# More of the first expert product ahead of the second, and one index lookup per route

## The chip, the cores and the metric

One program runs on one core of a Trainium2 chip. Times are device microseconds (us). TensorE (PE in the profile) multiplies matrices, VectorE (DVE) and ScalarE (ACT) work elementwise, GpSimd (POOL) issues gathers, and SyncE (SP) issues most transfers. Each engine works through its own list of instructions in order. A "tile" below is one weight block of 128 x 1024 float32, 512 KB.

## The reference

256 tokens of width 1024 pass two blocks of two layers each. The second block ends each layer with a layer of 16384 experts of which each token takes 8 x 16:

```python
q = (h @ w_pq).reshape(B, L, 8, 2, 128)
s = einsum("blhpd,hpkd->blhpk", q, peer_keys)       # 8 heads, 2 halves, 128 keys
sv, si = lax.top_k(s, 16)
cand = sv[..., 0, :, None] + sv[..., 1, None, :]     # 16 x 16 sums of a head
top_s, pos = lax.top_k(cand, 16)
eidx = take_along_axis(si0 * 128 + si1, pos)         # expert numbers
gate = softmax(top_s)
a = peer_down[eidx] @ h                              # first product, per expert
act = gate * gelu(a)
out = act @ peer_up[eidx]                            # second product
```

All else (retention, state-space scan, attention, pooling, Fourier mixing, feed-forward) is left alone by the change.

## The kernel before, in words

For the x tokens the expert layer is computed densely: all 128 tiles of `peer_down` (a *down* tile is 128 experts times 256 tokens, 24 matmuls), then gelu, then times a gate matrix that is zero for experts not chosen, then all 128 tiles of `peer_up` (an *up* tile, 24 matmuls that add to eight accumulators). This is `peer_dense(l)` from line 1549, once in each layer. For the context tokens of layer 0 the chosen rows are gathered instead (`peer_jobs`).

Every weight tile passes `Stream.run`: SP loads it into one of 4 stage buffers (line 338), ACT rounds it to a high half (line 314), DVE subtracts to get the low half (line 315, the *split*), and three matmuls per 128-row block multiply (lines 471 to 473). Splits are emitted up to three tiles ahead of the step that uses them. Beside the tiles run *background jobs* in lanes: each job carries a cost in steps, each step earns its lane a credit of 1, and jobs are emitted while the credit pays. When a lane is ended (`bg_end`), what is left is emitted at once. This gives the order in which instructions are emitted. From it and the dependencies the framework's scheduler fixes, at compile time, the order of each engine's list; it may move an instruction forward when it is ready and those emitted earlier are not.

In `peer_dense` the order of steps is: 16 tiles of `w_pq` (`dense_front`, line 1347), with the scores of a head after each pair; then AHEAD = 56 down tiles (line 1642 is their gelu); then pairs of one up and one down tile until all down tiles are done; then up tiles alone. In layer 0 the tiles of the next modulation are mixed into the up phase (`st.fill`).

The background jobs in lane 1 make the gate matrix. They are, in this order of emission: 8 *routes* of the first 128 tokens (one per head, `route`, line 1432, five jobs each at a cost of 0.4: two top-16 searches, the 16 x 16 sums with their own top 16, two lookups); a softmax and a transpose (lines 1575 and 1584); 32 *fours* (line 1587, cost 0.35: four one-hot matrices and one comparison on DVE at lines 1596 and 1598, then a product on PE at line 1604, copied by ACT at line 1605) mixed with the 8 routes of the other 128 tokens; then softmax, transpose and 32 fours for those. After each fourth four ACT sends 1 MB of gates to DRAM (line 1607). All have to be there before up tile 0: SP reads the gates back for eight tiles at a time (line 1647), `prep` multiplies them into a down result (line 1653) and makes its halves (lines 478 and 479).

The lookup in a route finds, for each of 16 chosen places, the key number in a list of 16: compare with 0..15 (line 1469), multiply by the numbers (line 1470), sum (lines 1473 and 1477), once for each half, after two conversions from integer (lines 1456 and 1465).

A down result needs a *slot* of 128 x 256 until its up tile; there are 56 in parts of other buffers. The halves of `prep` go into the first blocks of `y2`, the second operand of other stages, idle here.

Of the kernel before, what the change touches and what calls it, by code (L numbers as in the profile page):

```python
# [10 lines left out]
F32 = mybir.dt.float32  # L11
# [118 lines left out]
def dense_units(down, up):  # L130

    d = down.reshape(128, 128, 8, 128).transpose(0, 3, 2, 1).reshape(128, 128, 1024)
    u = up.reshape(128, 128, 1024)
    order = [d[i] for i in range(AHEAD)]
    for i in range(128):
        order += [u[i]] + ([d[i + AHEAD]] if i + AHEAD < 128 else [])
    return units(order)

# [29 lines left out]
N_ARENA = 14336  # L168
AHEAD = 56

# [193 lines left out]
def tile_model(ctx: ExitStack, tc: tile.TileContext, a: dict, out: bass.AP):  # L364
# [32 lines left out]
    def take(side, dtype=F32R):  # L397
        if dtype is F32R:
            place[side] = operands.tile([128, 2, NB, T], F32R, name=side, tag=side)
        else:  # L400
            place[side] = operands.tile([128, NB, T], F32, name=side + "f", tag=side)
    take("x2")
# [11 lines left out]
    gsm = keep.tile([128, DEPTH, 2, 2, NB], F32, name="gsm")  # L414
    ckv2 = keep.tile([128, 2, 2, T], F32R, name="ckv2")
    ckvh, ckvl = ckv2[:, 0], ckv2[:, 1]
# [8 lines left out]
    gates = keep.tile([128, 2, SLOTS], F32, name="gates")  # L425
    scratch = keep.tile([128, 512], F32, name="scratch")
    fgain = keep.tile([128, NB], F32, name="fgain")
# [603 lines left out]
    def modulation(l, c0, c1):  # L1031

        held = {}
        for i in range(4 * c0, 4 * c1):
            def go(w, oc=i // 4, kq=i % 4):
                if kq == 0:
                    held[0] = md_pool.tile([128, 512], F32, name="md")
                o = held[0][:4, :]
                for kk in range(2):
                    s, c = slice(kk * 512, (kk + 1) * 512), sc_s[:, 2 * kq + kk]  # L1040
                    PE.matmul(o, c, w[:, 0, s], start=kq == 0 and kk == 0, stop=False)
                    PE.matmul(o, c, w[:, 1, s], start=False, stop=kq == 3 and kk == 1)
                if kq == 3:
                    row = scratch[:4]
                    S.activation(row, o, AF.Copy)

                    def turn():
                        p = stat(8).rearrange("p (a b) -> p a b", b=2)
                        for j in range(4):
                            PE.matmul(p[:, j], row[:, j * 128:(j + 1) * 128], sel, start=True, stop=True)  # L1050
                        V.tensor_add(mods[:, l, oc * 4:oc * 4 + 4], p,
                                     bc(P("b_mod", l * 48 + oc * 4, 4)[:, :, None], [128, 4, 2]))
                    st.later(2, turn)
            st.w(go, (a[f"mod{l}"], i))
# [378 lines left out]
    def route(tt, hd, last=None, xi=None):  # L1433
# [3 lines left out]
        def part(o, *shape):  # L1437
            return shaped(scratch[:, o:], shape)
        sv, sif, siu = part(0, 2, 16), part(32, 2, 16), part(64, 2, 16).bitcast(U32)
        hs = slice(16 * hd, 16 * hd + 16)  # L1440
        e = part(112, 16)
        ts = part(96, 16) if xi is None else xi[:, 2, tt, hs]
        pu, au = part(128, 16).bitcast(U32), part(144, 2, 16).bitcast(U32)
        af, i12, zs = part(176, 2, 16), part(208, 2, 16), part(240, 1)
        cand, cf = part(256, 16, 16), part(256, 256)
        sq = [128, 16, 16]

# [7 lines left out]
        def pairs16():  # L1455
            put(V.tensor_copy(sif, siu))
            V.tensor_tensor(cand, bc(sv[:, 0][:, :, None], sq), bc(sv[:, 1][:, None, :], sq), op=OP.add)
            best16(ts, pu, cf)

            if xi is None:  # L1460
                V.tensor_scalar(e, ts, ts[:, 0:1], None, op0=OP.subtract)
                S.activation(e, e, AF.Exp, accum_out=zs)
            V.tensor_scalar(au[:, 0], pu, 4, None, op0=OP.logical_shift_right)
            V.tensor_scalar(au[:, 1], pu, 15, None, op0=OP.bitwise_and)
            V.tensor_copy(af, au)
            lookup(0)

        def lookup(half):
            V.tensor_tensor(cand, bc(af[:, half][:, :, None], sq), bc(iota16[:, None, :], sq), op=OP.is_equal)
            V.tensor_tensor(cand, cand, bc(sif[:, half][:, None, :], sq), op=OP.mult)  # L1470

        def chosen():
            put(V.tensor_reduce(i12[:, 0] if xi is None else xi[:, 0, tt, hs], cand, AX.X, OP.add))
            lookup(1)

        def gate():
            put(V.tensor_reduce(i12[:, 1] if xi is None else xi[:, 1, tt, hs], cand, AX.X, OP.add))
            if xi is None:
                V.scalar_tensor_tensor(idx[:, tt, hs], i12[:, 0], 128.0, i12[:, 1], op0=OP.mult, op1=OP.add)
                V.reciprocal(zs, zs)  # L1480
                V.tensor_scalar(gates[:, tt, hs], e, zs, None, op0=OP.mult)
        return [lambda: top(0), lambda: top(1), pairs16, chosen, gate]

# [74 lines left out]
    def peer_dense(l, filler=None, rate=0.0, between=None, middle=None):  # L1558
# [6 lines left out]
        hot = [shaped(w[:, 1024 * i:], (2, 4, 128)) for w in (AR, AR[:, 10240:]) for i in range(2)]  # L1565
        slots = [w[:, o:o + 256] for w in (AR[:, 2048:8192], flat(h2), flat(acc), rowbuf[3], AR[:, 12288:])
                 for o in range(0, w.shape[1], 256)]
        gd = nc.dram_tensor(f"gates{l}", (16, 128, 128, 16), F32, kind="Internal").ap()
# [47 lines left out]
        def routes(hd, tt):  # L1616
            return [(0.4, f, "") for f in route(tt, hd, None, xi)]

        def blocks(tt):
            return [(0.25, lambda: softmax(tt), ""), (1.0, lambda: turn(tt), "")] + [  # L1620
                (0.35, lambda b=b, g=g: four(b, g), "") for b in range(8 * tt, 8 * tt + 8) for g in range(4)]
        late = []
# [12 lines left out]
        def act(i):  # L1635
            return shaped(slots[i % AHEAD], (16, 16))

        def down(i):
            def go(w):
                p = mm(T)  # L1640
                proj(p, w)
                S.activation(slots[i % AHEAD], p, AF.Gelu_apprx_tanh)
            return go
# [5 lines left out]
        def prep(i):  # L1649
            if i % 8 == 0 and i < 120:  # L1650
                load(i // 8 + 1)
            w, f = act(i), slots[i % AHEAD]
            V.tensor_mul(w, w, held[i // 8][:, :, i % 8, :])
            halves(yh[:, i % 3], yl[:, i % 3], f)

        def up(i):
# [6 lines left out]
            def block(i, d, w):  # L1663
                s = slice(d * 128, d * 128 + 128)
                mm3(held["acc"][d // 2][:, d % 2], w[:, 0, s], w[:, 1, s], y2[:, :, i % 3],
                    i == 0 and d % 2 == 0, i == 127)
# [19 lines left out]
            return go if i < 126 else end  # L1686
        for i in range(AHEAD):
            if i == 24 and middle:
                middle()
            st.w(down(i), (W, i))  # L1690
        st.bg_end(1)
        k = AHEAD
        if filler:
            st.fill(filler, rate)
        for i in range(128):
# [3 lines left out]
            if i == 126:  # L1699
                st.w(up(i), (W, k), (W, k + 1))  # L1700
                break
            st.w(up(i), (W, k))
            k += 1
            if i + AHEAD < 128:
                st.w(down(i + AHEAD), (W, k))
                k += 1

# [141 lines left out]
```

## Time and profile before

| | |
|---|---|
| median of 3 runs | 4310.1 us (4305.79 to 4321.45) |
| profiled execution, and its span | 4318.26 us, 4316.5 us |
| mean granted TensorE clock | 0.968 of full |
| busy: PE, DVE, ACT, POOL | 4028.0, 3375.7, 2107.0, 383.0 us |
| share of the chain that ended last: PE, DVE, DMA | 58%, 29%, 5% |
| HBM | 966.94 MB read, 36.70 MB written |

Busy time of PE counts overlapped matmuls by their modelled ends, so that a PE which is starved for half of a gap can still look busy; the number of matmul records in a stretch says more.

### The profile page before, as it was taken

To read this page: it belongs to the slowest core of one execution; us is meant where nothing else is said; L and a number is where in the kernel's file an instruction comes from. 1 tells how busy PE (TensorE), PEld (TensorE's weight loads), DVE (VectorE), ACT (ScalarE), POOL (GpSimd) and SP (SyncE) were. 2 spreads that over 40 slices of the span, in tenths; PEclk is the share of its full clock that TensorE was granted. 3 is DMA by queue.
4 is the path that set the end of the run, shared out by engine and by line. 5 is a ranking of instruction groups with operands and counts; after the bars stand their busy time and mean duration, and the time that the engine had idled before them with its cause. 6 is when DMAs were issued, how large, how long until landed. Compare 5 with 4: busy or idle time off the path is not lost.

```text
span 4316.5 us, 77045 instructions
## 1 busy us (share of the span) xinstructions
PE 4028.0 (93%) x30546; PEld 3784.7 (88%) x30546; DVE 3375.7 (78%) x6606; ACT 2107.0 (49%) x3375; POOL 383.0 (9%) x260
## 2 busy tenths in 40 slices
PE   8998998999999999998988899999999989899999
PEld 6888887888899888997888889999988988899999
DVE  5679999979988887998899976665565799855555
ACT  5655445534444543455744445555445444444444
POOL 0001111122222112221100000000000000000000
PEclk9998998999999999999989999999999999999999
DMA  6666766788878678886754588776644445776654
GB/s 221 218 222 230 264 239 224 261 319 323 322 285 329 250 258 309 312 320 233 260 204 155 172 276 256 242 243 214 189 132 141 149 148 180 263 232 207 207 186 152
DMA packets 293305, 1008.66 MB, mean 234 GB/s; under 512 B 25744, under 2 KB 92944, under 8 KB 255184
## 3 DMA queue, kind: packets, MB, share of 16 engines
q1 hardware_dynamic: 250608, 698.32, 49.0%
q0 software_dynamic: 36864, 268.45, 16.3%
q10 hardware_dynamic: 5472, 36.97, 2.2%
q8 instruction: 240, 3.93, 0.4%
q14 instruction: 121, 0.99, 0.1%
HBM read 966.94 MB, written 36.70 MB: 233 GB/s over the span
## 4 chain that ended last, share of the span: by engine, by line
PE 58%; DVE 29%; DMA 5%; issue 5%; ACT 3%; POOL 0%; SPq 0%; DVEq 0%; ACTq 0%; POOLq 0%
PE mm L473 10%; PE mm L471 10%; PE mm L472 10%; DVE w L315 8%; PE ot L471 4%; PE ot L473 4%; PE ot L472 4%; PE mm L615 4%; DVE acc L1518 3%; DVE rows L1507 3%; DVE arena L1596 2%; DMA stage<-in_first 2%; ACT w L314 2%; DMA rows<-gates 1%; PE st L471 1%
## 5 line engine op out<-in xcount | busy, mean ns | idle before, releaser
L315 DVE TENSOR_TENSOR w<-stage,w 128x1024 fp32r<-128x1024 f32 (+1 forms) x1163 | 1406.3, 1214 | 590.9 <-ACT w L314 588.1
L314 ACT ACTIVATE w<-stage 128x1024 fp32r<-128x1024 f32 (+1 forms) x1163 | 1216.0, 1050 | 912.5 <-PE mm L473 353.4
L473 PE MATMUL mm<-x,w 128*128 128x256 f32 x4576 | 1301.6, 285 | 49.3 <-DVE w L315 49.0
L471 PE MATMUL mm<-x,w 128*128 128x256 f32 x4576 | 1311.5, 287 | 18.7 <-ACT x L481 9.0
L472 PE MATMUL mm<-x,w 128*128 128x256 f32 x4576 | 1297.8, 284 | 1.2 <-DVE x L482 1.1
L473 PEld LDWEIGHTS mm<-x,w 128*128 128x128 f32 x4576 | 876.7, 192 | 63.5 <-DVE w L315 61.1
L471 PEld LDWEIGHTS mm<-x,w 128*128 128x128 f32 x4576 | 878.7, 192 | 36.1 <-ACT x L481 9.6
L472 PEld LDWEIGHTS mm<-x,w 128*128 128x128 f32 x4576 | 877.6, 192 | 9.1 <-issue 4.3
L1501 POOL DMA_INDIRECT rows<-in_table,idx x256 | 382.8, 1495 | 1825.7 <-DVE acc L1518 1221.4
L473 PE MATMUL ot<-y,w 128*128 128x256 f32 (+1 forms) x1616 | 451.3, 280 | 5.5 <-DVE w L315 5.5
L471 PE MATMUL ot<-y,w 128*128 128x256 f32 (+1 forms) x1616 | 453.9, 281 | 1.8 <-DVE arena L1162 1.5
L472 PE MATMUL ot<-y,w 128*128 128x256 f32 (+1 forms) x1616 | 452.3, 280 | 1.3 <-DVE y L479 1.3
L473 PE MATMUL mm<-y,w 128*128 128x256 f32 x1456 | 420.1, 290 | 35.4 <-DVE w L315 35.2
L471 PE MATMUL mm<-y,w 128*128 128x256 f32 x1456 | 421.7, 290 | 19.5 <-ACT w L314 10.6
L472 PE MATMUL mm<-y,w 128*128 128x256 f32 x1456 | 415.0, 286 | 0.0
L1518 DVE SCALAR_TENSOR_TENSOR acc<-rows,dots,acc 128x1024 f32<-128x1024 f32 x254 | 324.7, 1278 | 0.4
L473 PEld LDWEIGHTS mm<-y,w 128*128 128x128 f32 x1456 | 282.3, 195 | 46.0 <-DVE w L315 44.9
L1507 DVE SCALAR_TENSOR_TENSOR rows<-rows,h 128x1024 f32<-128x1024 f32 x256 | 311.6, 1217 | 11.9 <-DMA rows<-in_table,idx 11.9
L471 PEld LDWEIGHTS ot<-y,w 128*128 128x128 f32 (+1 forms) x1616 | 302.0, 187 | 7.4 <-DVE arena L1162 2.2
L473 PEld LDWEIGHTS ot<-y,w 128*128 128x128 f32 (+1 forms) x1616 | 302.2, 187 | 7.0 <-DVE w L315 6.8
L471 PEld LDWEIGHTS mm<-y,w 128*128 128x128 f32 x1456 | 283.3, 195 | 24.6 <-ACT w L314 12.7
L472 PEld LDWEIGHTS ot<-y,w 128*128 128x128 f32 (+1 forms) x1616 | 302.2, 187 | 2.6 <-DVE y L479 1.5
(362 smaller groups left out, 6000.2 us busy)
## 6 DMA issues: line engine op xcount, KB each, us to landing
stage<-in_dense SPq DMA_DIRECT2D x512, 512.0 KB
stage<-in_first SPq DMA_DIRECT2D x392, 512.0 KB
stage<-in_mix SPq DMA_DIRECT2D x151, 512.0 KB
stage<-in_mod SPq DMA_DIRECT2D x96, 512.0 KB
gates<-rows ACTq DMA_DIRECT2D x32, 1024.0 KB
rows<-gates SPq DMA_DIRECT2D x32, 1024.0 KB
stage<-in_peer SPq DMA_DIRECT2D x50, 512.0 KB
stage<-in_first SPq DMA_DIRECT2D x32, 448.0 KB
```

What stands on the lines that cost most here:

```text
L314: nc.scalar.activation(h[:, :width], w, AF.Copy)
L315: self.last = nc.vector.tensor_sub(l[:, :width], w, h[:, :width].bitcast(F32))
L471: PE.matmul(o, sh, m[:, 0], start=start, stop=False, skip_group_check=True)
L472: PE.matmul(o, sh, m[:, 1], start=False, stop=False, skip_group_check=True)
L473: PE.matmul(o, sl, m[:, 0], start=False, stop=stop, skip_group_check=True)
L615: PE.matmul(held[0][:, b % 2], w[:, k * 128:k * 128 + 128], m[:, k0 + k], start=k == 0, stop=k == kb - 1, skip_group_check=True)
L1501: G.indirect_dma_start(out=b, out_offset=None, in_=table, in_offset=bass.IndirectOffsetOnAxis(ap=idx[:, tt, s:s + 1], axis=0))
L1507: queue(V.scalar_tensor_tensor(buf[i][:, :D], buf[i][:, :D], 1.0, h2[:, tt], op0=OP.mult, op1=OP.mult, accum_out=d), st.last)
L1518: queue(V.scalar_tensor_tensor(acc[:, tt], up, d, acc[:, tt], op0=OP.mult, op1=OP.add), st.last)
L1596: V.tensor_scalar(x[:, 0, j], iota, xt[:, 0, t + j:t + j + 1], xt[:, 2, t + j:t + j + 1], op0=OP.is_equal, op1=OP.mult)
```

## The change

AHEAD becomes 74 in layer 0 and 82 in layer 1. The added slots are two in the arena, 16 in the place of `y2` (taken as plain float32 for the time of the layer) and, in layer 1, eight in `rowbuf[2]`. The halves of `prep` go into `ckv2`, which gets a third block. The weights lie in DRAM as all down tiles, then all up tiles. The costs of the jobs become 0.5 (routes) and 0.45 (fours). The lookup compares and multiplies both halves in one instruction each, on the integers themselves, and sums them in one; the conversions go. `scratch` is twice as wide for it.

```diff
-    order = [d[i] for i in range(AHEAD)]
-    for i in range(128):
-        order += [u[i]] + ([d[i + AHEAD]] if i + AHEAD < 128 else [])
-    return units(order)
+    return units(list(d) + list(u))
 def param_layout():
...
-AHEAD = 56
+AHEAD = (74, 82)
...
-            place[side] = operands.tile([128, NB, T], F32, name=side + "f", tag=side)
+            place[side] = operands.tile([128, 2 * NB, T], F32, name=side + "f", tag=side)
...
-    ckv2 = keep.tile([128, 2, 2, T], F32R, name="ckv2")
+    ckv2 = keep.tile([128, 2, 3, T], F32R, name="ckv2")
...
-    scratch = keep.tile([128, 512], F32, name="scratch")
+    scratch = keep.tile([128, 1024], F32, name="scratch")
...
-                    row = scratch[:4]
+                    row = scratch[:4, :512]
...
         def part(o, *shape):
-        sv, sif, siu = part(0, 2, 16), part(32, 2, 16), part(64, 2, 16).bitcast(U32)
+        sv, siu = part(0, 2, 16), part(64, 2, 16).bitcast(U32)
         hs = slice(16 * hd, 16 * hd + 16)
-        af, i12, zs = part(176, 2, 16), part(208, 2, 16), part(240, 1)
+        i12, zs = part(208, 2, 16) if xi is None else xi[:, 0:2, tt, hs], part(240, 1)
-        sq = [128, 16, 16]
+        both = part(512, 2, 16, 16)
+        sq, bs = [128, 16, 16], [128, 2, 16, 16]
         def put(i):
...
         def pairs16():
-            put(V.tensor_copy(sif, siu))
-            V.tensor_tensor(cand, bc(sv[:, 0][:, :, None], sq), bc(sv[:, 1][:, None, :], sq), op=OP.add)
+            put(V.tensor_tensor(cand, bc(sv[:, 0][:, :, None], sq), bc(sv[:, 1][:, None, :], sq), op=OP.add))
...
-            V.tensor_copy(af, au)
-            lookup(0)
-        def lookup(half):
-            V.tensor_tensor(cand, bc(af[:, half][:, :, None], sq), bc(iota16[:, None, :], sq), op=OP.is_equal)
-            V.tensor_tensor(cand, cand, bc(sif[:, half][:, None, :], sq), op=OP.mult)
-        def chosen():
-            put(V.tensor_reduce(i12[:, 0] if xi is None else xi[:, 0, tt, hs], cand, AX.X, OP.add))
-            lookup(1)
+        def lookup():
+            put(V.tensor_tensor(both, bc(au[:, :, :, None], bs), bc(iota16[:, None, None, :], bs), op=OP.is_equal))
+            V.tensor_tensor(both, both, bc(siu[:, :, None, :], bs), op=OP.mult)
         def gate():
-            put(V.tensor_reduce(i12[:, 1] if xi is None else xi[:, 1, tt, hs], cand, AX.X, OP.add))
+            put(V.tensor_reduce(i12, both, AX.X, OP.add))
-        return [lambda: top(0), lambda: top(1), pairs16, chosen, gate]
+        return [lambda: top(0), lambda: top(1), pairs16, lookup, gate]
...
         hot = [shaped(w[:, 1024 * i:], (2, 4, 128)) for w in (AR, AR[:, 10240:]) for i in range(2)]
-        slots = [w[:, o:o + 256] for w in (AR[:, 2048:8192], flat(h2), flat(acc), rowbuf[3], AR[:, 12288:])
-                 for o in range(0, w.shape[1], 256)]
+        ahead = AHEAD[l]
+        slots = [w[:, o:o + 256] for w in [AR[:, 2048:8192], flat(h2), flat(acc), rowbuf[3]] + [rowbuf[2]] * l + [
+            AR[:, 9728:10240]] for o in range(0, w.shape[1], 256)]
+        slots += [View(lambda k=k: place["y2"][:, k]) for k in range(2 * NB)]
+        slots += [AR[:, o:o + 256] for o in range(12288, N_ARENA, 256)]
+        assert len(slots) == ahead
...
         def routes(hd, tt):
-            return [(0.4, f, "") for f in route(tt, hd, None, xi)]
+            return [(0.5, f, "") for f in route(tt, hd, None, xi)]
         def blocks(tt):
-                (0.35, lambda b=b, g=g: four(b, g), "") for b in range(8 * tt, 8 * tt + 8) for g in range(4)]
+                (0.45, lambda b=b, g=g: four(b, g), "") for b in range(8 * tt, 8 * tt + 8) for g in range(4)]
         def follow(hd):
...
         def act(i):
-            return shaped(slots[i % AHEAD], (16, 16))
+            return slots[i % ahead][:, :]
         def down(i):
             def go(w):
-                S.activation(slots[i % AHEAD], p, AF.Gelu_apprx_tanh)
+                S.activation(act(i), p, AF.Gelu_apprx_tanh)
         def load(j):
...
         def prep(i):
-            w, f = act(i), slots[i % AHEAD]
+            f = act(i)
+            w = shaped(f, (16, 16))
-            halves(yh[:, i % 3], yl[:, i % 3], f)
+            halves(ckvh[:, i % 3], ckvl[:, i % 3], f)
         def up(i):
             def start():
...
             def block(i, d, w):
-                mm3(held["acc"][d // 2][:, d % 2], w[:, 0, s], w[:, 1, s], y2[:, :, i % 3],
+                mm3(held["acc"][d // 2][:, d % 2], w[:, 0, s], w[:, 1, s], ckv2[:, :, i % 3],
             def go(w):
...
-        for i in range(AHEAD):
+        st.f(lambda: take("y2", F32))
+        for i in range(ahead):
-        k = AHEAD
         for i in range(128):
...
             if i == 126:
-                st.w(up(i), (W, k), (W, k + 1))
+                st.w(up(i), (W, 128 + i), (W, 129 + i))
-            st.w(up(i), (W, k))
-            k += 1
-            if i + AHEAD < 128:
-                st.w(down(i + AHEAD), (W, k))
-                k += 1
+            st.w(up(i), (W, 128 + i))
+            if i + ahead < 128:
+                st.w(down(i + ahead), (W, i + ahead))
+        st.f(lambda: take("y2"))
     def begin():
```

## Rows read from the trace of the kernel before


**Rows 1.** The page's 40 slices of 107.9 us: busy tenths.

```profile
PE   8998998999999999998988899999999989899999
DVE  5679999979988887998899976665565799855555
```

**Rows 2.** Stretches: length, busy us (records) of the engines; clock, DMA share, GB/s.

```profile
2205.00:2509.00 304.00, 261.96 (x2030) 250.05 (x2030) 299.05 (x977) 127.53 (x201) 0.94 (x1) 0.96 0.50 168
2509.00:2620.00 111.00, 102.92 (x808) 96.87 (x806) 75.57 (x123) 52.64 (x77) 0.00 (x0) 0.97 0.94 299
3430.00:3710.00 280.00, 243.83 (x1928) 231.34 (x1927) 275.00 (x908) 122.67 (x188) 0.00 (x0) 0.98 0.49 163
3710.00:3780.00 70.00, 66.74 (x563) 65.82 (x562) 50.88 (x94) 32.74 (x50) 0.00 (x0) 1.00 0.99 311
3820.00:4140.00 320.00, 320.00 (x2719) 320.00 (x2718) 182.03 (x227) 152.44 (x226) 0.00 (x0) 1.00 0.66 207
```

**Rows 3.** The first matmul of each block alone (line 471): the same columns.

```profile
2205.00:2509.00 304.00, 139.02 (x481) 93.97 (x480) 0.96 0.50 168
3430.00:3710.00 280.00, 128.39 (x454) 85.98 (x454) 0.98 0.49 163
```

**Rows 4.** DVE by form, 3430 to 3710 us: count, busy us, mean ns, idle.

```profile
L1596 DVE TENSOR_SCALAR arena<-cst,arena 128x128 f32<-128x128 f32 x256 | 73.4, 337 | 0.9 <-ACT arena L1585 0.9
L315 DVE TENSOR_TENSOR w<-stage,w 128x1024 fp32r<-128x1024 f32 x57 | 69.2, 1216 | 0.8 <-ACT w L314 0.8
L1598 DVE TENSOR_TENSOR arena<-cst,arena 128x512 f32<-128x512 f32 x64 | 43.6, 681 | 0.0
L1469 DVE TENSOR_TENSOR scratch<-scratch,cst 128x256 f32<-128x256 f32 x31 | 12.8, 414 | 0.1
L1456 DVE CAST scratch<-scratch 128x32 f32<-128x32 uint32 x15 | 2.6, 172 | 0.0
```

**Rows 5.** Waits of PE, 3430 to 3710 us: total, times, longest.

```profile
PE ot L1604 <- DVE arena L1598: 22.0, 34, 2.4
PE mm L473 <- DVE w L315: 8.5, 13, 1.3
```

**Rows 6.** DVE in order of time: start us, duration, line, names, shapes.

```profile
3494.78 1.22 DVE L315 TENSOR_TENSOR w<-stage,w 128x1024 fp32r<-128x1024 f32 x1
3495.91 0.42 DVE L1457 TENSOR_TENSOR scratch<-scratch 128x256 f32<-128x256 f32 x1
...
3502.57 0.41 DVE L1470 TENSOR_TENSOR scratch<-scratch 128x256 f32<-128x256 f32 x1
3502.89 0.09 DVE L1428 MATCH_VALUE_LOAD arena<-scratch,arena 128x8 f32 x1
...
3507.28 0.29 DVE L1575 TENSOR_TENSOR scratch<-arena 128x128 f32<-128x128 f32 x1
...
3512.57 1.10 DVE L1596 TENSOR_SCALAR arena<-cst,arena 128x128 f32<-128x128 f32 x4
3513.58 0.68 DVE L1598 TENSOR_TENSOR arena<-cst,arena 128x512 f32<-128x512 f32 x1
3514.19 1.11 DVE L1596 TENSOR_SCALAR arena<-cst,arena 128x128 f32<-128x128 f32 x4
```

**Rows 7.** ACT and its transfers around the last fours of layer 1, in order.

```profile
3661.80 0.38 ACT L1642 ACTIVATE rows<-mm 128x256 f32<-128x256 f32 x1
...
3708.64 0.38 ACT L1642 ACTIVATE rows<-mm 128x256 f32<-128x256 f32 x1
...
3709.85 0.60 ACT L1605 ACTIVATE rows<-ot 128x512 f32<-128x512 f32 x1
3710.48 0.33 ACTq L1607 DMA_DIRECT2D gates<-rows  x1
```

**Rows 8.** SP's queue there, in order: start, us until the last of xN.

```profile
3704.18 9.35 SPq L338 DMA_DIRECT2D stage<-in_dense  x4
3718.51 0.38 SPq L1647 DMA_DIRECT2D rows<-gates  x1
```

## The prediction

> **What bounds the kernel now.** I read the slices first [rows 1]: PE stands at 8 or 9 tenths all along, DVE at 9 in the slices that hold the two expert fronts (the 21st to 23rd, the 33rd and 34th), where PE falls back to 8 in most. Busy tenths of PE mislead, so next I counted matmul records by stretch [rows 2]. The last row of that group is a stretch of up and down tiles with PE never idle: 320 us for 2719 records, 0.1177 us each, and 24 of them make a tile of 2.825 us. By that price the front of layer 1 (3430 to 3710 us) holds 1928 x 0.1177 = 226.9 us of PE work in 280 us: 53.1 us are lost. Layer 0 (2205 to 2509) holds 238.9 us in 304: 65.1 us lost. The first matmuls of blocks, eight to a tile, show it as tiles [rows 3]: 454 are 57 tiles in 280 us, 4.9 us each. In the stretches behind them the loss is 3.7 us (layer 1) and at most 15.9 us (layer 0, where wider matmuls of the modulation are in the count). So some 138 us are at stake in the two expert layers, and nothing elsewhere is touched in size.
>
> In both fronts DVE is busy 98% (275.0 of 280 and 299.05 of 304 us) with transfers at half load: DVE is the bound. The list by form says with what [rows 4]: 57 splits and 64 fours (256 + 64 instructions), the rest routes. PE's waits name the same two, fours and splits [rows 5]. Start to start [rows 6], a split takes 3495.91 - 3494.78 = 1.13 us and a four 3514.19 - 3512.57 = 1.62 us. Of 280 us that leaves 280 - 57 x 1.13 - 64 x 1.62 = 112 us, 7.0 us for each of 16 routes. The clearest sight of the loss is ACT's list at the end of the front [rows 7]: no down tile ends between 3661.80 and 3708.64, 47 us, while fours follow one another; at full speed 16 tiles would have passed. When the last four is copied (3709.85), only some 47 of the 56 down tiles are done, and nine are left to cover the gates' way through DRAM. Those nine do cover it nearly: 3.7 us are lost in the 70 us behind.
>
> **What the change is worth: the lead.** Until the last four, time is DVE's work: all background jobs, plus 1.13 us per tile. PE's share is 2.825 us per tile plus 64 products of 8 records (0.94 us each). Each tile more that PE can run before the last four costs DVE 1.13 us there and takes 2.825 us from the PE-bound rest: a gain of 1.70 us per tile, as long as DVE stays the bound. How many more? I followed the credit step by step. With costs of 0.4 and 0.35 the last four is emitted at down step 44; with 0.5 and 0.45 at step 59. The trace has it executed at tile 47, three behind its step, as far as splits run ahead. So 15 tiles more, in either layer: 74 and 82 differ only in what is left behind step 59, 14 and 22 tiles, more than the nine that suffice now. 15 x 1.70 = 25.4 us per layer.
>
> Does DVE stay the bound? By step, new: while routes alone run (2 jobs of 1.34 us a step) DVE needs 3.8 us against PE's 2.83; where routes and fours mix (1.43 fours, 0.71 jobs) 4.4 against 4.2; in the last fours (2.2 a step) 4.7 against 4.9. There PE is the bound for 15 steps, and DVE idles 0.18 x 15 = 3 us. I take these off: 22.5 us.
>
> **The lookup.** Gone are, per route, two compares, two multiplies and two sums of 256 and two conversions; new are one each of 512. Rows: 256 elements of two operands take 0.32 us to the next start (3502.57 to 3502.89), 512 take 0.61 (3513.58 to 3514.19); a conversion lasts 172 ns and hides some 0.09 of it. 6 x 0.32 + 2 x 0.08 - 3 x 0.61 = 0.25 us, times 16 is 4 us per layer. No row shows a compare of uint32 with float32. The nearest are the float compare (0.414 us) and the conversion, which reads uint32 at no visible cost; I take the float rate. Bounds: at half rate two instructions cost 0.55 us more each, 17.6 us per layer; and below the sum nothing, for the elements remain. The 16 routes of the context tokens save 4 us more on DVE in layer 0, where PE is the bound; I count 1 of it.
>
> The Trainium skill ("VectorE: DVE Perf Modes", Side-by-side: where the cycles go for N=2048 bf16) gives every instruction about 158 cycles of start and fill beside its elements, at 0.96 GHz some 165 ns (an estimate from that page); five instructions fewer would save 0.82 us per route, 13 per layer, and the whole sum would grow by 18. The rows say 0.03 us between 2 x 0.32 and 0.61, so most of such a start overlaps the instruction ahead; I stay with them.
>
> **What moves at no cost.** The new order in DRAM keeps 512 KB blocks whole; ups and downs alternate in the same loads. The halves' new place has three blocks, as the old one. Slots in the place of `y2` are free then: its last readers are matmuls ahead of the front. Taking it back needs the last `prep` to have ended; the next writer comes behind up 127 on PE, so I cost it 0; if it were late, the price is one `prep` chain, under 2 us. The first readback of gates is moved past 18 (or 26) more weight loads on SP and as many gelus on ACT; POOL has none. Now SP stands for it from 3713.53 to 3718.51 [rows 8], with four loaded tiles (11.3 us of PE) as cover. More results done ahead also means that gates can be read back earlier for ten blocks of eight instead of seven. Behind the front 311 GB/s move where PE's tiles need 0.524 MB per 2.825 us, 186 GB/s; a 1.05 MB block fills the spare 125 GB/s for 8.4 us. Layer 1 lost 3.7 us to about seven such blocks, so three more cost 1.6, and in layer 0 some 4; against it 14 tiles now run before the modulation's loads join. I take 0 (bounds -6 and +8).
>
> **Sum.** 2 x (22.5 + 4) + 1 = 54 us, plus or minus 20. The profiled execution took 4318.3 us, 1.8 beyond its span: 4264. It was 8.2 us (0.19%) above the median of 4310.1, to which I give the same 54: 4256 us.
>
> The granted clock in the fronts is 0.96 and 0.98, beside 1.00 in the full stretch [rows 2]: a mix of 2.4 and 1.2 GHz, after gaps of PE. That loses 304 x 0.04 + 280 x 0.02 = 18 us of PE's work, free as long as DVE is the bound. If the drops stay, some fall into steps where PE now decides: up to 18 us less, 4274. The Trainium skill ("TensorE: Matmul & The Clock Gate", Part 1: The HAM clock gate) has the array at half clock after idling and at full after sustained work. By it fewer gaps mean fewer drops; the rows agree in that only the gapless stretch is at 1.00.
>
> **Rivals.**
> - *PE never starves.* If the scheduler weaves fours evenly, idle shrinks to some 12 us in each front (its start, and the two softmax chains): 41 + 53 = 94 us, 4216. For it: the per-step demands above are near each other. Against: routes alone stay DVE-bound by 1 us a step for some 30 steps.
> - *The lead is not used.* The scheduler moves what is ready; if routes, now with a shorter chain of dependent steps, and fours run as early as before, the last four is again at tile 47 and only 9 us of lookups are won: 4301. For it: DVE's list strays from the order of emission already (PE's drought of 47 us is as long as 29 fours). Against: that drought comes from fours emitted by step 44 that waited for routes, and later splits cannot pass them.
> - *Integers are slow.* 54 - 35 = 19 us: 4291.
> - *SP waits for the gates* (slower). SP's list is fixed at compile time. If the first readback is placed by a time at which the gates are written too early, all weight loads behind it stand. Loaded tiles cover 11.3 us; each further tile of misplacement costs 2.8 us in each layer, and from ten tiles beyond the cover (39 us of wait, 28 lost) the gain is gone; at fifteen it is 84 lost in two layers, 4340. For it: SP does stand there now, 5 us. Against: that is an eighth of what is needed.
>
> **How the numbers follow.** Forecast 0.61, PE full 0.12, lead unused 0.10, integers 0.07, SP 0.10. About 0.5% (21.6 us) can be told from no change: faster takes the first two and half of the integers, 0.77; same 0.13; slower 0.10. The likeliest alone: 4236 to 4278. The range reaches to the rivals at either side: 4214 to 4302.
>
> **What would show it.** The last four's copy at down tile 60 to 63 (wrong at 47 to 52); it comes some 12 us later than now, counted from the front's start; idle of PE by records in the same stretches near 25 and 37 us; DVE still above 95% there; lookups of 512 at 0.6 us; SP's wait for the first readback under 11 us. The forecast is wrong if DVE falls below 90% with PE idle, or if the alternating stretch takes more than 2.83 us per tile.

## The result, and the profile after

The changed kernel takes 4249.9 us (median of 4 runs, 4244.6 to 4252.5), the kernel before 4311.6 (4305.8 to 4321.5): a ratio of 0.9853, 95% interval 0.9832 to 0.9874, 62 us less. The profiled execution took 4248.41 us, its span 4246.6. Two single executions below were slow, at 10.9 and 12.9 ms (one with the lookup in the dense routes, one of the kernel before), and are in no ratio.

The page's 40 slices show it first: from the 8th on, PE is at 8 tenths in two (the 19th and the 21st), where it was so in six [rows 1]; DVE is as full in the fronts as before.

```profile
PE   8998998999999999998989999999999999999999
DVE  5678999979987888898899987666565799865555
```

Next the stretches as in [rows 2]: the front of layer 0 (from 57 us ahead of the first gelu to the last four) and 70 us behind it, the same of layer 1 (from 37 us ahead), and a stretch of tiles with PE never idle.

```profile
2184.00:2507.00 323.00, 300.12 (x2445) 291.18 (x2445) 316.48 (x916) 150.98 (x235) 0.94 (x1) 0.98 0.55 184
2507.00:2577.00 70.00, 62.95 (x507) 59.59 (x506) 46.07 (x83) 31.85 (x48) 0.00 (x0) 1.00 0.91 298
3387.00:3679.00 292.00, 275.33 (x2283) 267.92 (x2282) 290.09 (x852) 142.56 (x218) 0.00 (x0) 1.00 0.57 184
3679.00:3749.00 70.00, 68.01 (x569) 67.01 (x568) 49.30 (x91) 32.59 (x51) 0.00 (x0) 1.00 0.99 311
3780.00:3990.00 210.00, 210.00 (x1788) 210.00 (x1787) 120.00 (x150) 99.87 (x148) 0.00 (x0) 1.00 0.67 208
```

The last row gives the price of a record again, 210 / 1788 = 0.1174 us; I keep 0.1177. The fronts lose 323 - 2445 x 0.1177 = 35.2 us and 292 - 2283 x 0.1177 = 23.3 us, where 65.1 and 53.1 were lost. The two stretches behind lose 10.3 and 3.0 us (before, over 70 us: 10.0 and 3.7). That is 59.7 us out of the two fronts. The two profiled spans differ by 4316.5 - 4246.6 = 69.9, so some 10 us more were won elsewhere (below) or are scatter between two executions, and nothing was given back behind the fronts. DVE is still busy 98 and 99%: the bound has not changed hands, PE only gets more done under it. The granted clock in the fronts rose from 0.96 and 0.98 to 0.98 and 1.00.

The tiles in the fronts, as first matmuls of blocks [rows 3]; here the stretches begin 54 and 37 us ahead of the first gelu:

```profile
2187.00:2507.00 320.00, 171.49 (x609) 114.74 (x609) 0.98 0.56 185
3387.00:3679.00 292.00, 161.27 (x572) 107.78 (x572) 1.00 0.57 184
```

572 / 8 = 71.5 tiles in 292 us, 4.1 us each, where it was 4.9. Which of them are down tiles up to the last four, ACT's gelus count (line 1639, the former L1642; two of the records are table loads), from the first gelu to the last four's copy in layers 0 and 1:

```profile
2240.80:2506.60 265.80, 25.92 (x63) 0.98 0.55 185
3424.10:3679.40 255.30, 25.94 (x63) 1.00 0.58 190
```

61 tiles in both layers, where it was 47 (L1642 before, with two table loads again):

```profile
2264.20:2509.10 244.90, 20.56 (x49) 0.97 0.50 169
3467.10:3710.50 243.40, 20.56 (x49) 0.98 0.49 167
```

DVE's list by form in the front of layer 1, to be laid beside [rows 4]:

```profile
L313 DVE TENSOR_TENSOR w<-stage,w 128x1024 fp32r<-128x1024 f32 x72 | 87.9, 1222 | 0.1
L1593 DVE TENSOR_SCALAR arena<-cst,arena 128x128 f32<-128x128 f32 x256 | 74.2, 356 | 0.0
L1595 DVE TENSOR_TENSOR arena<-cst,arena 128x512 f32<-128x512 f32 x64 | 44.8, 700 | 0.0
L1467 DVE TENSOR_TENSOR scratch<-scratch 128x512 f32<-128x512 f32 x16 | 11.1, 691 | 0.3
L1466 DVE TENSOR_TENSOR scratch<-scratch,cst 128x512 f32<-128x512 uint32 x16 | 11.0, 690 | 0.2
L1470 DVE TENSOR_REDUCE arena<-scratch 128x32 f32<-128x512 f32 x16 | 10.9, 684 | 0.2
```

Splits went from 57 to 72; fours are as many as before; the compare on integers (L1466) takes 690 ns, the float multiply of the same size 691. PE's waits there [rows 5]: the wait for fours' matrices has gone from 22.0 to 4.4 us, that for splits is unchanged.

```profile
PE mm L471 <- DVE w L313: 8.6, 8, 2.9
PE ot L1601 <- DVE arena L1595: 4.4, 8, 0.9
```

One lookup in DVE's order of time, beside the old one in [rows 6]:

```profile
3448.70 1.22 DVE L313 TENSOR_TENSOR w<-stage,w 128x1024 fp32r<-128x1024 f32 x1
3449.84 0.69 DVE L1466 TENSOR_TENSOR scratch<-scratch,cst 128x512 f32<-128x512 uint32 x1
3450.56 0.69 DVE L1467 TENSOR_TENSOR scratch<-scratch 128x512 f32<-128x512 f32 x1
3451.29 0.69 DVE L1470 TENSOR_REDUCE arena<-scratch 128x32 f32<-128x512 f32 x1
3451.89 0.08 DVE L1425 MATCH_VALUE_LOAD scratch<-scratch,arena 128x8 f32 x1
```

ACT at the end of layer 1's front [rows 7], gelus and fours side by side, and then SP's queue [rows 8]:

```profile
3672.20 0.39 ACT L1639 ACTIVATE y2f<-mm 128x256 f32<-128x256 f32 x1
...
3676.94 0.39 ACT L1639 ACTIVATE y2f<-mm 128x256 f32<-128x256 f32 x1 [0.33 <-PE mm L471]
...
3678.76 0.60 ACT L1602 ACTIVATE rows<-ot 128x512 f32<-128x512 f32 x1 [0.50 <-PE ot L1601]
3679.40 0.33 ACTq L1604 DMA_DIRECT2D gates<-rows  x1
3680.65 0.38 ACT L1639 ACTIVATE y2f<-mm 128x256 f32<-128x256 f32 x1 [1.29 <-PE mm L471]
```

```profile
3672.02 8.06 SPq L336 DMA_DIRECT2D stage<-in_dense  x4
3685.62 0.38 SPq L1644 DMA_DIRECT2D rows<-gates  x1
```

Where no down tile had ended for 47 us [rows 7], one now does every 3.4 to 5.3 us with a four or more beside it; the longest gap left between two gelus of this front is 20 us (3632.79 to 3652.91), shortly before these. SP stands for the first readback from 3680.08 to 3685.62, 5.5 us.

### The profile page after: what moved, and what is told of

Its sections match the earlier page's. It is cut to its first block, busy times and chain, and to the rows that moved or that the text cites. A ratio compares the mean times of both kernels' runs of the same rounds, so it can differ in the third digit from the quotient of the medians.

```text
span 4246.6 us, 76805 instructions
## 1 busy us (share of the span) xinstructions
PE 4000.0 (94%) x30546; PEld 3765.7 (89%) x30546; DVE 3352.9 (79%) x6366; ACT 2106.4 (50%) x3373; POOL 396.1 (9%) x260
## 3 DMA queue, kind: packets, MB, share of 16 engines
q0 software_dynamic: 36864, 268.45, 16.4%
## 4 chain that ended last, share of the span: by engine, by line
PE 55%; DVE 30%; DMA 6%; issue 5%; ACT 3%; POOL 1%; SPq 0%; DVEq 0%; ACTq 0%; POOLq 0%
PE mm L471 9%; DVE w L313 9%; PE mm L469 9%; PE mm L470 9%; PE ot L470 4%; PE ot L469 4%; PE ot L471 4%; PE mm L613 3%; DVE rows L1500 3%; DVE acc L1511 3%; DMA rows<-gates 2%; DMA stage<-in_first 2%; DVE arena L1593 2%; ACT w L312 2%; PE st L469 1%
## 5 line engine op out<-in xcount | busy, mean ns | idle before, releaser
L471 PE MATMUL mm<-x,w 128*128 128x256 f32 x4576 | 1301.3, 285 | 42.5 <-DVE w L313 42.2
L469 PE MATMUL mm<-x,w 128*128 128x256 f32 x4576 | 1307.5, 286 | 14.5 <-ACT x L479 9.0
L1494 POOL DMA_INDIRECT rows<-in_table,idx x256 | 395.9, 1547 | 1800.5 <-DVE acc L1511 1123.3
L471 PE MATMUL ot<-ckv,w 128*128 128x256 f32 x1536 | 433.0, 282 | 4.3 <-DVE w L313 4.2
L470 PE MATMUL ot<-ckv,w 128*128 128x256 f32 x1536 | 433.3, 282 | 1.2 <-DVE ckv L477 1.2
L469 PE MATMUL ot<-ckv,w 128*128 128x256 f32 x1536 | 430.9, 281 | 0.0
L471 PEld LDWEIGHTS ot<-ckv,w 128*128 128x128 f32 x1536 | 289.9, 189 | 5.6 <-DVE w L313 5.6
L469 PEld LDWEIGHTS ot<-ckv,w 128*128 128x128 f32 x1536 | 289.9, 189 | 4.4 <-ACT arena L1639 0.3
L470 PEld LDWEIGHTS ot<-ckv,w 128*128 128x128 f32 x1536 | 289.5, 188 | 2.7 <-DVE ckv L477 1.4
```

The costliest lines, as they stand in the source:

```text
L469: PE.matmul(o, sh, m[:, 0], start=start, stop=False, skip_group_check=True)
L470: PE.matmul(o, sh, m[:, 1], start=False, stop=False, skip_group_check=True)
L471: PE.matmul(o, sl, m[:, 0], start=False, stop=stop, skip_group_check=True)
L1494: G.indirect_dma_start(out=b, out_offset=None, in_=table, in_offset=bass.IndirectOffsetOnAxis(ap=idx[:, tt, s:s + 1], axis=0))
```

## The experiments

All were timed in turns with the kernel before on the same chip; its median was 4312.8 us in the runs of the first four experiments, 4308.6 in those of the next four and 4308.3 in those of the last two. The three groups ran on three chips, so kernels of different groups are better compared by their ratios. For each kernel the table has the down tile at which the last four is copied (layers 0 and 1), the time that PE loses in the fronts, counted by records as above, and what it loses in the 70 us behind.

| | tile | lost in fronts | lost behind | ratio, 95% |
|---|---|---|---|---|
| before | 47, 47 | 65.1, 53.1 | 10.0, 3.7 | |
| lookup alone | 47, 47 | 58.0, 47.7 | 8.0, 3.4 | 0.9951 (0.9937 to 0.9964) |
| all but the lookup | 61, 61 | 42.6, 29.8 | 9.4, 2.3 | 0.9912 (0.9898 to 0.9925) |
| tiles ahead, old costs | 47, 47 | 57.9, 47.7 | 5.0, 4.8 | 0.9978 (0.9968 to 0.9988) |
| changed kernel | 61, 61 | 35.2, 23.3 | 10.3, 3.0 | 0.9853 (0.9832 to 0.9874) |
| 66 ahead | 61, 61 | 34.9, 23.4 | 8.9, 5.5 | 0.9862 (0.9847 to 0.9877) |
| costs alone | 56, 56 | 49.6, 37.5 | 18.1, 15.0 | 0.9963 (0.9947 to 0.9980) |
| costs 0.65, 0.40 | 70, 69 | 20.7, 14.6 | 12.0, 3.3 | 0.9812 (0.9789 to 0.9835) |
| 0.7, 0.4 / 0.7, 0.45 | 74, 76 | 16.4, 11.3 | 17.0, 0.8 | 0.9798 (0.9780 to 0.9815) |
| 0.6, 0.4 / 0.7, 0.45 | 66, 76 | 27.0, 10.9 | 9.6, 1.3 | 0.9821 (0.9799 to 0.9843) |

**The two halves of the change.** First the kernel before with the new lookup alone:

```diff
...
+            put(V.tensor_tensor(both, bc(au[:, :, :, None], bs), bc(iota16[:, None, None, :], bs), op=OP.is_equal))
+            V.tensor_tensor(both, both, bc(siu[:, :, None, :], bs), op=OP.mult)
...
```

> The kernel before with the new lookup alone (56 tiles ahead, costs 0.4 and 0.35). Lead theory: the last four stays at down tile 47, so only the lookups are won: 4 us in each expert layer, and the 13 us by which the stage with the context tokens' routes came earlier in the changed kernel's profile, if they are the lookup's: some 4291 us. If those 13 us are scatter between two profiles: 4303. Lookup theory (the single lookup, with its shorter chain, is what moves the fours and gives most of the gain): 4255 to 4270.

Measured: 4290.0 us (4287.4 to 4298.4). Then the changed kernel with the old lookup in its place (the same lines taken back):

> The changed kernel with the old lookup in every route. Lead theory: the last four at down tile 61 as in the changed kernel, 8 us lost in the expert layers, and 13 more if the earlier context stage is the lookup's: 4258 to 4271 us. Lookup theory: the routes hold the fours back again and most of the gain goes: 4290 or more.

Measured: 4270.6 us (4269.9 to 4278.0). The parts, -22.8 and -42.2 us, add up to -65 where the whole gave -61.7 against its own runs of the kernel before: within the scatter they simply add. The fronts of the second lose 22.5 and 23.3 us less than before.

**What of the lead matters: the tiles ahead, or the costs?** The changed kernel with the old costs:

```diff
-            return [(0.5, f, "") for f in route(tt, hd, None, xi)]
+            return [(0.4, f, "") for f in route(tt, hd, None, xi)]
-                (0.45, lambda b=b, g=g: four(b, g), "") for b in range(8 * tt, 8 * tt + 8) for g in range(4)]
+                (0.35, lambda b=b, g=g: four(b, g), "") for b in range(8 * tt, 8 * tt + 8) for g in range(4)]
```

> The changed kernel with the old costs of jobs, 0.4 and 0.35; 74 and 82 tiles still run ahead. Lead theory: the last four is emitted at step 44 again and copied at tile 47, so that the longer lead only leaves more tiles behind the fours, where none was short: the time of the lookup alone, some 4290 us. Cover theory (what helps is that more down tiles stand ready behind the fours while the gates go through DRAM): as the changed kernel, 4250.

Measured: 4302.9 us (10 runs, 4291.7 to 4308.6). The gelus from the first one to the last four, by the same view as above:

```profile
2242.30:2489.10 246.80, 20.60 (x49) 0.95 0.49 168
3443.00:3682.00 239.00, 20.60 (x49) 0.97 0.50 170
```

47 tiles, as in the kernel with the lookup alone, and the same loss in the fronts: 18 and 26 tiles more of room, which the jobs do not spread into, are worth nothing. The lead theory had 4290 us, though: that it is 13 us slower than the lookup alone, timed on the same chip, stays open. Its profiled execution, the fastest of the ten (4291.7 us), does not show where. It differs from the lookup alone by the longer lead and by the moves that came with it (the halves, the slots, the order in DRAM).

The converse, the kernel before with the new costs alone (the same two lines the other way round):

> The kernel before with the costs 0.5 and 0.45 alone: 56 tiles ahead, old slots, old order in DRAM, old lookup. The fours left at step 55 are emitted at once behind the last down tile. Theory that the tiles ahead are needed as room (to spread over, and as cover for the gates): all 56 tiles before the last four instead of 47, 9 x 1.70 = 15 us per layer won, but no tile is left beside the gates' way through DRAM, about 15 us per layer lost: 4305 us, plus or minus 8. Rival, the costs alone do it: 4271 us, as with all of the change but the lookup. Idle of PE behind the last four would be 15 us or more in each layer by the first, under 5 by the second.

Measured: 4293.8 us (10 runs, 4285.1 to 4308.6), lower than expected by 11, but by both terms of that theory. Its profiled execution was the slowest of the ten (4308.6). The fronts lose 15.5 and 15.6 us less than before: nine tiles more, at 1.70 each 15.3. And the stretches behind lose 8.1 and 11.3 us more, since no down tile is left to cover the gates. The rows are the two stretches of 70 us, and PE's longest waits in each, layer 0 first:

```profile
2529.00:2599.00 70.00, 59.38 (x441) 54.36 (x442) 49.43 (x92) 29.72 (x44) 0.00 (x0) 0.93 0.93 293
...
3717.00:3787.00 70.00, 57.49 (x467) 56.45 (x467) 48.84 (x98) 27.76 (x43) 0.00 (x0) 0.93 0.97 294
```

```profile
PE ot L471 <- ACT y L478: 5.9, 1, 5.9
```

```profile
PE ot L471 <- ACT y L478: 9.9, 1, 9.9
```

PE waits for the halves of the first up tile, 5.9 and 9.9 us; I had priced the whole way of the gates at 15; 8.1 and 11.3 are what it cost.

**How many tiles ahead?** 66 in both layers:

```diff
-AHEAD = (74, 82)
+AHEAD = (66, 66)
...
-        assert len(slots) == ahead
+        slots = slots[:ahead]
```

> The changed kernel with 66 tiles ahead in both layers, costs of jobs as changed. Lead theory: the last four is copied at tile 61 as before; five tiles, 14 us, stand behind it, and the gates need about 15 us from that copy to up tile 0: at most 1 to 4 us lost in each layer, 4250 to 4258 us. Cover theory: 8 and 16 tiles fewer cost 1.7 us each, 4290.

Measured: 4249.9 us (4247.8 to 4257.9). Between 66 and 74 or 82 there is no difference: past the last four, five tiles of cover do.

**Spreading the jobs further.** The changed kernel with other costs:

```diff
-            return [(0.5, f, "") for f in route(tt, hd, None, xi)]
+            return [(0.65, f, "") for f in route(tt, hd, None, xi)]
-                (0.45, lambda b=b, g=g: four(b, g), "") for b in range(8 * tt, 8 * tt + 8) for g in range(4)]
+                (0.4, lambda b=b, g=g: four(b, g), "") for b in range(8 * tt, 8 * tt + 8) for g in range(4)]
```

> The changed kernel with the cost of route jobs 0.65 instead of 0.5 and of fours 0.40 instead of 0.45. The last four is then emitted at down step 68 instead of 59. Lead theory (each down tile more before the last four is worth 2.83 - 1.13 = 1.70 us while DVE is the bound): last four copied at tile 70 or 71, 9 tiles x 1.70 = 15 us per layer, 30 us in all, 4220 us; in layer 0 only 3 or 4 of 74 tiles are then left to cover some 15 us of gates through DRAM, which takes back about 5 us: 4225 us. Idle of PE by records in the fronts would fall from 34 and 23 us to under 20 and 12. Rival, PE is the bound by now (what idle is left lies in the softmax chains and at the start): last four at tile 70 but later by 2.8 us for each tile, 4245 to 4255 us. Rival, the scheduler's order holds the last four at tile 61: 4250 us.

Measured: 4223.2 us (4219.8 to 4236.6). The lead theory holds beyond the change: with the last four at tiles 70 and 69 the median is another 27 us lower. The two were not timed together; by the ratios, whose intervals just overlap, it is 18 us, and by the loss in the fronts 23. Its two fronts:

```profile
2182.00:2517.00 335.00, 320.83 (x2670) 313.85 (x2670) 328.33 (x929) 163.76 (x255) 0.94 (x1) 1.00 0.58 191
...
3376.00:3682.00 306.00, 293.98 (x2476) 290.38 (x2475) 302.44 (x862) 151.95 (x234) 0.00 (x0) 0.99 0.58 191
```

Layer 0 loses 14.5 us less than the changed kernel, nine tiles at 1.61. Layer 1 loses 8.7 less for eight tiles, 1.09 each: there the price falls. Where does it end? Two more, which differ by layer (0 first, then 1):

```diff
+            return [((0.7,0.7)[l], f, "") for f in route(tt, hd, None, xi)]
+                ((0.4,0.45)[l], lambda b=b, g=g: four(b, g), "") for b in range(8 * tt, 8 * tt + 8) for g in range(4)]
```

> The changed kernel with costs of routes and fours of 0.7 and 0.4 in layer 0 (last four emitted at step 72 of 74, so at the end of the down tiles) and 0.7 and 0.45 in layer 1 (step 75 of 82). Beside the kernel with 0.65 and 0.40 in both (4223 us; last four at tile 70 and 69, 19.4 and 14.6 us of PE idle by records left in the fronts, 12.2 and 3.6 us lost in the 70 us behind). Lead theory with its cover: layer 0 wins 4 more tiles x 1.70 = 6.8 us and loses as much again since no tile is left beside the gates' way through DRAM (loss behind the last four 18 to 20 us); layer 1 wins 6 x 1.70 = 10 us as far as the 14.6 us of idle allow, so 5 to 10: 4213 to 4218 us. Rival, PE is the bound by now and a later last four only shortens the cover: idle of layer 1 stays at 12 to 15 us, total 4223 to 4232 us.

Measured: 4224.1 us (4220.2 to 4226.9), the rival's range and not the 4213 to 4218 of the lead theory. The same with 0.6 for the routes of layer 0:

> The changed kernel with 0.6 and 0.4 in layer 0 (last four emitted at step 64, executed at tile 66: eight tiles left as cover for the gates) and 0.7 and 0.45 in layer 1 (step 75 of 82). Lead theory: layer 0 gives back 4 x 1.70 = 6.8 us of lead against tile 70 and wins back 2 us of loss behind the last four; layer 1 as in the kernel with 0.7 and 0.45 there: 4217 to 4223 us. Rival, in layer 0 what counts is the cover, not the lead past tile 66: 4213 us. Rival, layer 1 is bound by PE: 4228 us.

Measured: 4232.0 us (4224.2 to 4243.6), nearest to the rival in which PE bounds layer 1 (4228). Neither is below 4223 by more than the runs scatter. The rows of the first, the front of layer 0, the 70 us behind it and the front of layer 1, say why:

```profile
2185.00:2527.00 342.00, 331.86 (x2766) 325.00 (x2765) 335.62 (x938) 169.14 (x265) 0.94 (x1) 1.00 0.58 193
2527.00:2597.00 70.00, 60.69 (x450) 55.97 (x449) 49.13 (x91) 30.45 (x44) 0.00 (x0) 0.90 0.93 298
3378.00:3700.00 322.00, 312.23 (x2640) 309.20 (x2639) 310.38 (x868) 160.56 (x248) 0.00 (x0) 0.99 0.58 192
```

In layer 0 (last four at tile 74, none left) the front loses 16.4 instead of 20.7 us, and the stretch behind it 17.0 instead of 12.0: cover and lead trade one for one. In layer 1 seven tiles more bring 3.3 us, 0.5 each, and DVE is busy 310.38 of 322 us, 96%: what is left to win there is about used up. So both halves of the expectation show in the rows, each at a smaller size; the rival (PE bound) is nearer to layer 1 from tile 69 on, though 11.3 us are still lost there. The kernel with 0.6 for layer 0 loses 27.0 us in that front (tile 66), the one with 0.65 and 0.40 loses 20.7 (tile 70), and 9.6 against 12.0 behind; in layer 1 it loses 10.9 against 14.6, and 1.3 against 3.3 behind. By these counts it should stand where the one with 0.65 and 0.40 does, and its interval overlaps that one's.

**Where the lookup's 23 us came from.** The new lookup in one kind of route only:

```diff
+    def route(tt, hd, last=None, xi=None):
+        return (route_two if xi is not None else route_one)(tt, hd, last, xi)
```

`route_one` is the new route, `route_two` the old; `xi` is None for the context tokens.

> The kernel before with the new lookup in the 16 routes of the context tokens alone (the gathered ones of layer 0); the routes of the x tokens look up as before. The lookup in all routes took 22.8 us off, where the sum had 9 (4 in each dense front and 1 here). If the excess lies in the context stretch, as a shift of the loads between 570 and 840 us suggests: 4299 to 4306 us. If the context routes are hidden behind PE, as the sum had it: 4312 us.

Measured: 4298.9 us (12 runs, 4288.7 to 4310.4; ratio 0.9981, 0.9969 to 0.9994). The other way round:

> The kernel before with the new lookup in the routes of the x tokens alone (32 routes, two layers); the context tokens' routes as before. By the sum 4 us per layer: 4305 us. If the whole 22.8 us of the lookup lie in the dense fronts (fewer instructions in the chain of each route, each start costing more than the overlap of independent ones showed): 4290 us.

Measured: 4300.7 us (ten of its eleven runs at 4293.5 to 4310.2; ratio 0.9982, 0.9967 to 0.9997), between the two expectations. By the medians about 10 us lie in the context's routes and 8 in the dense ones; by the intervals of the ratios each can be anything from 1 or 3 us to 14. In the first of the two, counted by the same of SP's weight loads in both traces, the gain over the kernel before goes from 2 us at the 194th load (625 us) to 11 at the 250th (884 us). The stretch from the 174th to the 250th load, in the kernel before and in this one:

```profile
543.60:883.80 340.20, 305.36 (x2054) 277.08 (x2055) 313.90 (x643) 166.60 (x270) 57.93 (x43) 0.93 0.69 251
543.80:872.80 329.00, 296.72 (x2054) 269.18 (x2055) 310.71 (x613) 167.12 (x270) 58.95 (x44) 0.95 0.71 259
```

All twelve traces agree in this: between these two loads lie 339.4 to 342.7 us in the four kernels with the old lookup in the context's routes, and 329.1 to 335.2 in the eight with the new one. Only five of the sixteen routes run there (570 to 683 us); over the eleven ahead of them the gain moves by less than 2 us. DVE's busy time falls by 3.2 of the 11 us, its idle time from 26.3 to 18.3. Three stretches inside, of the kernel before, then of this one:

```profile
600.00:650.00 50.00, 49.63 (x292) 43.59 (x291) 50.00 (x129) 21.00 (x37) 7.50 (x6) 0.97 0.68 244
650.00:700.00 50.00, 37.45 (x249) 35.09 (x248) 43.80 (x109) 20.54 (x34) 5.03 (x4) 0.80 0.57 205
700.00:760.00 60.00, 53.50 (x396) 48.66 (x395) 58.19 (x96) 35.40 (x55) 11.27 (x8) 0.97 0.68 251
```

```profile
600.00:650.00 50.00, 49.34 (x305) 42.40 (x305) 49.92 (x124) 22.68 (x39) 7.83 (x6) 0.99 0.71 256
650.00:700.00 50.00, 38.73 (x276) 37.04 (x276) 48.54 (x108) 23.59 (x38) 5.43 (x5) 0.86 0.62 222
700.00:760.00 60.00, 55.55 (x393) 49.16 (x393) 58.59 (x98) 35.24 (x57) 11.64 (x9) 1.00 0.71 260
```

DVE is busy 50.00 of 50 us, with the dots of the gathered rows, splits and the scan's own work, and 58.19 of 60; PE alone, as the sum had it, is not the bound. The first stretch does not tell the two apart, since PE shows 49.63 there too. In the middle one neither is full, and PE's two longest waits of the kernel before there are for a split on DVE and a rounding on ACT:

```profile
PE mm L473 <- DVE w L315: 6.4, 3, 3.3
PE mm L471 <- ACT w L314: 3.7, 1, 3.7
```

The middle stretch has the granted clock at 0.80 before and 0.86 here.

## Why the prediction was right

**The bound.** That DVE bounds the fronts and PE is fed too few tiles beside it was right, and the order of experiments shows it: over the whole front, moving jobs later is worth 1.6 to 1.7 us per tile up to tile 61, and to tile 70 in layer 0; in layer 1 it is 1.1 up to tile 69 and 0.5 up to tile 76, where DVE has fallen to 96%. Part of it lies ahead of the first gelu, where routes run as well: from the first gelu on, all of the change but the lookup saves 18.8 and 21.5 us for its 14 tiles, 1.3 and 1.5 each.

**The lead.** Predicted were 15 tiles at 1.70, less 3: 22.5 us per layer. Measured without the lookup: 14 tiles, 22.5 and 23.3 us less lost, 42.2 us on the clock. The last four came at tile 61 (predicted 60 to 63), idle at 35.2 and 23.3 us (predicted 37 and 25). That 22.5 was met so closely is partly luck: one tile fewer came, and the 3 us in which DVE was to idle did not (from the first gelu to the last four it stands 1.4 and 1.3 us). The rival "PE never starves", with 12 us of idle in each front, was not reached; later jobs came near it (16.4 and 11.3). The rival "the lead is not used" doubted that the scheduler keeps the order of emission. For the costs it does: the tile followed the emission step by 1 to 3 in all kernels whose last four is emitted by its own credit.

**Its time.** The last four was to come 12 us later from the front's start. From the first gelu it is 255.3 - 243.4 = 11.9 us in layer 1, but 265.8 - 244.9 = 20.9 in layer 0. The lookup alone brings it 4.4 us forward in layer 1 and puts it 1.9 back in layer 0. There its gain comes earlier: ahead of the first gelu, where the first routes stand beside the last rows of the context, 57.2 - 367 x 0.1177 = 14.0 us are lost before and 5.1 with the lookup alone.

```profile
2207.00:2264.20 57.20, 47.95 (x367) 46.92 (x366) 57.16 (x202) 21.81 (x34) 0.94 (x1) 0.91 0.50 162
2196.00:2252.90 56.90, 53.51 (x440) 52.67 (x439) 52.93 (x143) 26.38 (x40) 0.94 (x1) 0.97 0.54 177
```

It is the dense lookup that does this: 5.1 us are lost there with it alone, 15.5 with the context's alone. Why nothing more is gained from the first gelu on in layer 0 is open.

**The lookup.** The term that failed: 9 us predicted, 22.8 measured (17.6 as the sum of the two halves). The instructions were at the forecast rate, 684 to 691 ns, integers too, and the rival "integers are slow" falls. But start to start the three of the lookup shown above take 0.72, 0.73 and 0.60 us, not 0.61 each, as the second and third need the one ahead; where they follow each other directly their saving alone is smaller still. Two things were missed. With the lookup alone the fronts lost 7.1 and 5.4 us less, instead of 4 each. And the context's routes gave some 10 us, which with these 12.5 make up the 22.8: I counted 1 of 4 us there because PE was taken for the bound. The rows above show DVE full in two stretches of three. That about 10 us came of work worth 4 is not explained by that work, of which five routes of sixteen lie where the gain is; most of it is less waiting on both engines. The clock fell less there (0.80 to 0.86 over 50 us is 3 us of PE's work), but whether that is a cause of the shorter stretch or follows from the shorter waits is not shown. By the Trainium skill ("VectorE: DVE Perf Modes", Side-by-side: where the cycles go for N=2048 bf16) a start of about 165 ns for each of five instructions saved would, by the estimate in the prediction, have made 13 us per layer. The dense lookups alone gave 8 us in two layers (at most 14 by the interval): the runs do not bear that size out.

**What was costed at nothing.** The stretches behind lose 10.3 and 3.0 us against 10.0 and 3.7, so the halves in `ckv2`, the slots in `y2` and the order in DRAM show no cost there. That they cost nothing at all is not shown: these moves and the longer lead are all that sets the kernel with old costs apart from the lookup alone, and it took 13 us more with the same loss in the fronts. SP's wait for the first readback was 5.5 us, half of the cover that I gave it; the rival in which it grows past 39 us had nothing for it.

**The clock.** Up to 18 us were feared if PE's half-speed spells stayed. Instead the granted clock rose to 0.98 and 1.00 in the fronts, where PE now waits less (for fours 4.4 us instead of 22.0 in layer 1). The rows did not say quite what the prediction read in them, that only the gapless stretch is at 1.00: the 70 us behind the front of layer 1 are at 1.00 too, with 3.7 us lost. The forecast of 4256 was missed by 6 us: by the medians the lookup gave some 14 more than its term and the lead some 3 less, and the two parts together are 3 more than the whole.

## What to carry to other kernels

Where background work is paced by costs, the last job's place among the foreground's tiles is the number to look for: each tile moved ahead of it is worth the difference between the two engines' prices for a tile, until the starved engine is full or the tiles behind no longer cover the chain that follows. Buffers for more tiles ahead are worth nothing until the pacing uses them, and pacing alone is worth less without tiles for cover. Here 0.65 and 0.40 beat both kernels: 4223.2 us, 18 us (by ratios) to 27 us (by medians) below the changed one.

Whether an engine has slack is to be read for each stretch in which an edit acts, also for the part of the edit that looks small: the page's slices showed DVE at 9 in the context's stretch too, from the 4th to the 8th [rows 1].

## What the runs showed that was not expected

- On DVE, the second and third instruction of a lookup (512 elements), which need the one ahead, start 0.71 to 0.73 us after it wherever they follow it directly (29 pairs in the changed kernel); an instruction that does not need it starts after 0.60 us (3451.29 to 3451.89).
- A compare that reads uint32 on one side and float32 on the other ran at the float rate: 690 ns against 691.
- In 50 us of the context's stretch (650 to 700 us) PE's granted clock was 0.80, a mix of 2.4 and 1.2 GHz, while PE waited 7.0 us for DVE and 5.5 for ACT. The four traces with the old lookup in the context's routes have 0.80 to 0.83 there, the eight with the new one 0.86 to 0.90.
